# First stage of a two-layer decoder trunk: positions and rope tables first, casts ahead of the block inputs, four more raw buffers, filler matmuls

## The chip, the cores and the metric

The kernel runs on one core of a Trainium2 chip. The metric is the device time of one execution in microseconds (us); the figure used is the median of several executions. The engines of the core are TensorE (PE in the profile, its weight loads PEld), VectorE (DVE), ScalarE (ACT), GpSimd (POOL) and SyncE (SP, which here only issues DMAs).

## What is computed

Two decoder layers on 256 tokens of width 1024, in f32. Each layer modulates its input by a shift and a scale that come from the conditioning vector c, projects it, runs a convolution branch and a retention branch, and then a feed-forward part (dense in layer 0, 8 experts in layer 1).

```python
c_act = jax.nn.silu(c)
for l in range(DEPTH):                                   # DEPTH = 2
    ada = c_act @ w_ada[l] + b_ada[l]
    shift1, scale1, gate1, shift2, scale2, gate2 = [a[:, None, :] for a in jnp.split(ada, N_ADA, axis=-1)]
    h = x * (1.0 + scale1) + shift1
    mix = token_mixer(h, positions, w_in[l], ...)        # proj = h @ w_in; conv_a, conv_b, q, k, v, ... = split(proj)
    x = layer_norm(DEEPNORM_ALPHA * x + gate1 * mix, ln1_g[l], ln1_b[l])
    h = x * (1.0 + scale2) + shift2
    ff = swiglu(h, ...) if l % 2 == 0 else moe_swiglu(h, ...)
    x = layer_norm(DEEPNORM_ALPHA * x + gate2 * ff, ln2_g[l], ln2_b[l])
```

In the mixer, `u = conv_a * sigmoid(conv_b)` feeds the convolution, and q and k are turned by `cos(ang)` and `sin(ang)` with `ang = positions * inv_freq`.

## The kernel before

The weights are streamed once from HBM in units of 128 x 2048 f32 (1 MB), by DMAs that SP issues in the order of the program. They land in a ring of `NWF` = 4 raw buffers `wf`. A weight that TensorE multiplies is split in two halves of 128 x 1024: ScalarE casts the high part (`wh`), VectorE subtracts to get the low part (`wl`), both in rings of `NWS` = 6, and every product is the sum of three matmuls: wh with hH, wh with hL, and wl with hH, where hH and hL are the same two parts of the layer's input. The program is written in a fixed order: `split_to` emits the casts and subtractions some pieces ahead of their use, `issue_dma` emits the next DMA as soon as a raw buffer is free in program order. Each engine runs its own instructions strictly in that order.

The first stage (lines 707 to 717, the loop over `START`) computes conv_a and conv_b of layer 0. Its contraction over 1024 rows is cut into 8 blocks, k = 0 to 7. For block k two units arrive: `adat` (unit a_k) and `s` (unit s_k).

- a_k: VectorE multiplies its two halves by `cb`, the broadcast of silu(c), with a running sum (line 264), which gives shift and scale of the 128 rows of block k in `adac`; line 685 adds the bias.
- `first_h(k)` then makes the modulated input of the block from the transposed x (`xT`). For k = 0 VectorE (line 688), ScalarE (690) and VectorE (691) do it, for k = 1 to 7 GpSimd does all three steps (lines 695, 697, 698).
- s_k is cast and split (lines 1696 and 1698), and `products(k)` (line 674) issues 48 matmuls of 128 x 256: 2 halves, 8 PSUM regions, 3 products. All 8 PSUM banks stay open over the 8 blocks, and after block 7 `A_drain` empties them into `upad`.

Ahead of the stage, `setup` fetches c, makes `cb` with two matmuls and two Silu, and interleaves the DMAs of `cols` (all small per-channel columns), `xT`, `pos` (positions) and the first units. `rope_tables` (from line 1085; VectorE and ScalarE) stands in the program between block 0 and block 1. What follows the stage (`setup_late`, the q and k units `ws`, the units `v` and `g`, and the convolution on VectorE and ScalarE) is the same text in both kernels.

Of the kernel before, what the change touches and what calls it, by code (L numbers as in the profile page):

```python
# [20 lines left out]
P = 128  # L21
T = 256
# [94 lines left out]
def _emit(tc, ctx, a):  # L117
# [6 lines left out]
    small.tile([P, 32], F32, name="padl", bufs=1)  # L124
# [22 lines left out]
    class Unit:  # L147
        kind = None

        def __init__(self, src, n, fn, raw=False, look=LEAD, slot=("stream", "wf", NWF)):  # L150
            self.src, self.n, self.fn, self.raw = src, n, fn, raw
            self.look, self.slot, self.lo = look, slot, {}
            self.issued, self.before = False, None
# [21 lines left out]
    state = {}  # L175
# [275 lines left out]
    def mixer(l, raws, bound, fill=(), tail=()):  # L451
# [4 lines left out]

        def open_pool():
# [8 lines left out]
            R["rH"] = R["p"].tile([P, 16, T], F32R, name="rH")  # L466
            R["rL"] = R["p"].tile([P, 16, T], F32R, name="rL")
            pool.memset(R["upad"][:, :, 0:30], 0.0)
            R["taps"] = col("taps", l * 8 * CK, 8 * CK).rearrange("p (a b) -> p a b", a=8)
# [183 lines left out]
        def S_unit(k):  # L653
            def fn(s, w, wl):
                have.setdefault(k, []).append((w, wl))
                products(k)
            u = Unit(W["s"][k], 2048, fn)
            u.look = 1
            return u

        def products(k):
            if ("h", k) not in have:
                return
            if k == 0 and "A" not in R:
                R["A"] = [mm_bank() for _ in range(4)] + [tp_bank(), tp_bank(), sc_bank(), sc_bank()]
            hi, lo = state["hH"][:, k, :], state["hL"][:, k, :]
            while have.get(k):
                w, wl = have[k].pop(0)
                s = have[k, "s"] = have.get((k, "s"), -1) + 1
                for i in range(8):  # L670
                    o = R["A"][i][:, s * T:(s + 1) * T]
                    ws, wr = w[:, i * P:(i + 1) * P], wl[:, i * P:(i + 1) * P]
                    for n, (p, q) in enumerate(((ws, hi), (ws, lo), (wr, hi))):
                        pe.matmul(o, p, q, start=k == 0 and s == 0 and n == 0, stop=k == 7 and s == 1 and n == 2,
                                  skip_group_check=True)
                    if k == 7 and s == 1:
                        A_drain(i)

        def first_h(k):
            def fn():  # L680
# [5 lines left out]
                f = R["hp"].tile([P, T], F32, name="fh", tag="rot0", bufs=2)  # L686
                if k == 0:
                    dve.tensor_scalar(f, mixc["xT"][:, k, :], adac[:, 0, 8 + k:9 + k], adac[:, 0, k:k + 1],
                                      op0=ALU.mult, op1=ALU.add)
                    act.copy(state["hH"][:, k, :], f)  # L690
                    dve.tensor_tensor(state["hL"][:, k, :], f, state["hH"][:, k, :], op=ALU.subtract)
                    have["h", k] = True
                    products(k)
                    return
                pool.tensor_scalar(f, mixc["xT"][:, k, :], adac[:, 0, 8 + k:9 + k], adac[:, 0, k:k + 1],
                                   op0=ALU.mult, op1=ALU.add)
                pool.tensor_copy(state["hH"][:, k, :], f)
                pool.tensor_tensor(state["hL"][:, k, :], f, state["hH"][:, k, :], op=ALU.subtract)
                have["h", k] = True
                products(k)  # L700
            return fn

        if l == 0:
# [381 lines left out]
    def rope_tables(p):  # L1085
# [20 lines left out]
        dve.scalar_tensor_tensor(n, ang, -1.0, ang, op0=ALU.mult, op1=ALU.max)  # L1106
        dve.tensor_scalar(n, n, -1.0, math.pi / 2, op0=ALU.mult, op1=ALU.add)
        act.activation(cos, n, AF.Sin)
# [559 lines left out]
    def issue_dma(upto=None):  # L1668
        while st["dma"] < (len(units) if upto is None else upto):
# [8 lines left out]
            u.wf = p.tile([P, 2048], F32, name="wf", tag=tag, bufs=bufs)  # L1678
            for o in range(0, u.n, 1024 if u.idx < 2 else u.n):
# [6 lines left out]
    def split_to(i, eng=dve):  # L1686
        while st["split"] <= min(i, len(subs) - 1):
# [3 lines left out]
            if not u.raw:  # L1691
                w = stream.tile([P, 1024], F32R, name="wh", tag="wh", bufs=NWS)
                wl = stream.tile([P, 1024], F32R, name="wl", tag="wl", bufs=NWS)
                m = u.width(s)
                src = u.wf[:, s * 1024:s * 1024 + m]
                act.copy(w[:, 0:m], src)  # L1696
# [132 lines left out]
```

## Time and profile before

| | us |
|---|---|
| median of 3 runs | 1744.8 (1744.21 to 1747.59) |
| profiled execution | 1747.31 |
| its span | 1745.4 |
| PE busy in the span | 1693.2 (97%) |
| DVE busy | 1548.4 (89%) |
| ACT busy | 1159.6 (66%) |
| POOL busy | 53.3 (3%) |

Of 40 equal slices of the span TensorE is busy for 9 tenths or more in all but the first and the last; in the first (0 to 43.6 us) it is 6 tenths. The span is what the profiler recorded from the first instruction to the last; the execution's own time is 1.9 us longer. Matmuls are pipelined, so the distance between two starts tells TensorE's pace better than the duration shown for one of them.

### The profile page before, as it was taken

To read this page: it belongs to the slowest core of one execution; us is meant where nothing else is said; L and a number is where in the kernel's file an instruction comes from. 1 tells how busy PE (TensorE), PEld (TensorE's weight loads), DVE (VectorE), ACT (ScalarE), POOL (GpSimd) and SP (SyncE) were. 2 spreads that over 40 slices of the span, in tenths; PEclk is the share of its full clock that TensorE was granted. 3 is DMA by queue.
4 is the path that set the end of the run, shared out by engine and by line. 5 is a ranking of instruction groups with operands and counts; after the bars stand their busy time and mean duration, and the time that the engine had idled before them with its cause. 6 is when DMAs were issued, how large, how long until landed. Compare 5 with 4: busy or idle time off the path is not lost. (4 is left out here: it accounts for less than half of the span.)

```text
span 1745.4 us, 23910 instructions
## 1 busy us (share of the span) xinstructions
PE 1693.2 (97%) x8896; PEld 1424.0 (82%) x8896; DVE 1548.4 (89%) x2144; ACT 1159.6 (66%) x1634; POOL 53.3 (3%) x50
## 2 busy tenths in 40 slices
PE   6999999999999999999999999999999999999996
PEld 5988877669997798888887788888888888887885
DVE  7699989877787779999878999899999999898996
ACT  3566787644444565667645878778887878787783
POOL 5300000000000000000000000000000000000001
PEclk8999999999999999999999999999999999999998
DMA  9644458876789544455577799899998999898892
GB/s 358 260 164 161 166 208 295 309 294 230 299 303 353 205 171 161 154 192 174 189 301 290 304 333 389 306 383 361 370 363 329 382 354 383 310 393 308 323 351 86
DMA packets 71389, 491.59 MB, mean 282 GB/s; under 512 B 7985, under 2 KB 8753, under 8 KB 14178
## 3 DMA queue, kind: packets, MB, share of 16 engines
q1 hardware_dynamic: 69410, 484.29, 74.0%
q0 software_dynamic: 1568, 5.45, 0.9%
q8 instruction: 72, 1.18, 0.3%
q14 instruction: 51, 0.42, 0.1%
q10 hardware_dynamic: 288, 0.26, 0.0%
HBM read 488.92 MB, written 1.05 MB: 281 GB/s over the span
## 5 line engine op out<-in xcount | busy, mean ns | idle before, releaser
L1698 DVE TENSOR_TENSOR wl<-wf,wh 128x1024 fp32r<-128x1024 f32 x819 | 977.4, 1220 | 80.1 <-ACT wh L1696 66.0
L1696 ACT CAST wh<-wf 128x1024 fp32r<-128x1024 f32 x819 | 840.9, 1049 | 169.3 <-PE ps_mm L140 102.7
L140 PE MATMUL ps_mm<-wh,hgH 128*128 128x512 f32 x704 | 283.5, 403 | 0.0
L140 PE MATMUL ps_mm<-wh,hgL 128*128 128x512 f32 x704 | 275.8, 392 | 0.0
L140 PE MATMUL ps_mm<-wl,hgH 128*128 128x512 f32 x704 | 275.2, 391 | 0.2 <-DVE wl L1698 0.2
L480 ACT ACTIVATE tap<-upad,cols 128x256 f32<-128x256 f32 x300 | 129.6, 501 | 83.9 <-DVE ycv L492 83.8
L140 PE MATMUL ps_mm<-hHn,wh 128*128 128x256 f32 x576 | 163.5, 284 | 0.0
L140 PE MATMUL ps_mm<-hHn,wl 128*128 128x256 f32 x576 | 163.0, 283 | 0.0
L140 PE MATMUL ps_mm<-hLn,wh 128*128 128x256 f32 x576 | 163.0, 283 | 0.0
L140 PEld LDWEIGHTS ps_mm<-wh,hgL 128*128 128x128 f32 x704 | 132.5, 188 | 28.2
L140 PEld LDWEIGHTS ps_mm<-wl,hgH 128*128 128x128 f32 x704 | 132.9, 189 | 26.7 <-issue 1.0
L140 PEld LDWEIGHTS ps_mm<-wh,hgH 128*128 128x128 f32 x704 | 132.6, 188 | 26.0 <-issue 1.0
L140 PE MATMUL ps_mm<-wh,mb 128*128 128x512 f32 (+1 forms) x476 | 145.8, 380 | 0.0
L140 PEld LDWEIGHTS ps_mm<-hHn,wh 128*128 128x128 f32 x576 | 110.6, 192 | 0.4 <-issue 0.2
L140 PEld LDWEIGHTS ps_mm<-hLn,wh 128*128 128x128 f32 x576 | 110.6, 192 | 0.4 <-issue 0.2
L140 PEld LDWEIGHTS ps_mm<-hHn,wl 128*128 128x128 f32 x576 | 110.6, 192 | 0.0
L140 PEld LDWEIGHTS ps_mm<-wh,mb 128*128 128x128 f32 x476 | 87.9, 188 | 17.5 <-issue 1.5
L492 DVE TENSOR_TENSOR ycv<-ycv,tap 128x1024 f32<-128x1024 f32 (+1 forms) x90 | 93.9, 1043 | 5.6 <-ACT tap L480 4.2
L140 PE MATMUL ps_mm<-wl,mb 128*128 128x512 f32 (+1 forms) x238 | 89.8, 377 | 0.0
L140 PE MATMUL ps_mm<-wh,hHn 128*128 128x512 f32 x208 | 84.9, 408 | 0.0
L140 PE MATMUL ps_mm<-wh,hLn 128*128 128x512 f32 x208 | 81.4, 391 | 0.5 <-DVE hLn L392 0.5
L264 DVE SCALAR_TENSOR_TENSOR wf<-wf,cb 128x1024 f32<-128x1024 f32 x64 | 78.1, 1255 | 3.5 <-ACT cb L224 2.0
(306 smaller groups left out, 2851.9 us busy)
## 6 DMA issues: line engine op xcount, KB each, us to landing
wf<-moe_gu SPq DMA_DIRECT2D x176, 1024.0 KB, 7.1
wf<-moe_d SPq DMA_DIRECT2D x75, 1024.0 KB, 6.3
wf<-adat SPq DMA_DIRECT2D x31, 1024.0 KB, 5.9
wf<-ws SPq DMA_DIRECT2D x24, 1024.0 KB, 5.0
wf<-ffn_gu SPq DMA_DIRECT2D x20, 1024.0 KB, 6.1
wf<-v SPq DMA_DIRECT2D x16, 1024.0 KB, 4.9
wf<-g SPq DMA_DIRECT2D x16, 1024.0 KB, 5.0
wf<-f SPq DMA_DIRECT2D x16, 1024.0 KB, 4.9
```

Source lines behind the costliest of these rows:

```text
L140: pe.matmul(out, lhsT, rhs, start=start, stop=stop)
L264: dve.scalar_tensor_tensor(wj, wj, 1.0, state["cb"], op0=ALU.mult, op1=ALU.mult, accum_out=adac[:, l, c0:c0 + 1])
L480: act.activation(t[:, c - c0, :], u[:, c, j:j + T], AF.Copy, scale=taps[:, c, j:j + 1])
L492: dve.tensor_tensor(y, y, prod[j][:, 0:n, :], op=ALU.add)
L1696: act.copy(w[:, 0:m], src)
L1698: eng.tensor_tensor(wl[:, 0:m], src, w[:, 0:m], op=ALU.subtract)
```

## The change

In words:

- `pos` is fetched by the first DMA of ScalarE's queue, and only the first 105 of the 777 columns of `cols` (c, b_ada, inv_freq) are fetched at the start; the other 672 go with unit s_4. `xT` is fetched in pieces of 1, 1, 2 and 4 blocks, ahead of s_0, s_1, s_2 and s_3.
- `rope_tables` is emitted in `setup`, ahead of the bias copy and of a_0. Two of its VectorE steps become one on ScalarE (Abs, and a Sin with bias and scale).
- GpSimd's three steps per block go: ScalarE writes hH straight from `xT` (Identity with scale and bias) and f once more in f32, VectorE subtracts (`low_h`). The low part of block k is emitted after the split of s_k.
- For k of 1 and above, the two casts of s_k stand ahead of hH of block k in ScalarE's order (`early_cast`).
- `products` goes over all 8 regions with one of the three products, then with the next, the one with hL last; only the last half of block 7 keeps the three together.
- a_2, s_2, a_3 and s_3 land in four buffers of their own (the room of rH and rL, which are not in use yet), so that eight units can be under way at first.
- 2 and 9 small matmuls that nobody reads are issued on TensorE around the two that make `cb`.

```diff
+WARM = (2, 9)
+XQ = {0: (0, 1), 1: (1, 2), 2: (2, 4), 3: (4, 8)}
...
     def setup():
...
+        act.dma_start(mixc["pi"], a["pos"].partition_broadcast(P))
         sp.dma_start(row, a["c"])
+        sp.dma_start(cols[:, 0:NCOL0], a["cols"][:, 0:NCOL0])
         pool.memset(one, 1.0)
+        pool.memset(half_pi, math.pi / 2)
+        make_identity(nc, ident)
+        ps = sc_bank()
+        for _ in range(WARM[0]):
+            mm(ps[:, 0:P], one, one, True, True)
         for q in range(2):
             ps = tp_bank()
             mm(ps, one, row[:, q * 512:(q + 1) * 512], True, True)
             act.activation(cb[:, q * 512:(q + 1) * 512], ps, AF.Silu)
-        sp.dma_start(cols, a["cols"])
+        ps = sc_bank()
+        for _ in range(WARM[1]):
+            mm(ps[:, 0:P], ident, ident, True, True)
         st["go"] = True
-        issue_dma(1)
-        sp.dma_start(mixc["xT"][:, 0:2, :], a["xT"][:, 0:2, :])
-        issue_dma(2)
-        sp.dma_start(mixc["pi"], a["pos"].partition_broadcast(P))
-        issue_dma(3)
-        sp.dma_start(mixc["xT"][:, 2:8, :], a["xT"][:, 2:8, :])
-
-        make_identity(nc, ident)
+        issue_dma(8)
+        rope_tables(state["hp0"], half_pi)
...
         def S_unit(k):
             def fn(s, w, wl):
+                if ("f", k) in R:
+                    split_to(st["cur"] + 1)
+                    low_h(k, R.pop(("f", k)))
...
-                for i in range(8):
+                end = k == 7 and s == 1
+                turns = [(i, n) for i in range(8) for n in range(3)] if end else \
+                    [(i, n) for n in range(3) for i in range(8)]
+                for i, n in turns:
                     o = R["A"][i][:, s * T:(s + 1) * T]
...
+                    p, q = ((w, hi), (wl, hi), (w, lo))[n]
...
+        def early_cast(u):
+            for s in range(2 if u.issued else 0):
+                w = stream.tile([P, 1024], F32R, name="wh", tag="wh", bufs=NWS)
+                wl = stream.tile([P, 1024], F32R, name="wl", tag="wl", bufs=NWS)
+                act.copy(w, u.wf[:, s * 1024:(s + 1) * 1024])
+                u.w[s] = (w, wl)
...
+                xk, s, b = mixc["xT"][:, k, :], adac[:, 0, 8 + k:9 + k], adac[:, 0, k:k + 1]
+                act.activation(state["hH"][:, k, :], xk, AF.Identity, bias=b, scale=s)
                 if k == 0:
...
-                pool.tensor_scalar(f, mixc["xT"][:, k, :], adac[:, 0, 8 + k:9 + k], adac[:, 0, k:k + 1],
-                                   op0=ALU.mult, op1=ALU.add)
-                pool.tensor_copy(state["hH"][:, k, :], f)
-                pool.tensor_tensor(state["hL"][:, k, :], f, state["hH"][:, k, :], op=ALU.subtract)
...
+                    act.activation(f, xk, AF.Identity, bias=b, scale=s)
+                    R["f", k] = f
...
+        def low_h(k, f):
+            dve.tensor_tensor(state["hL"][:, k, :], f, state["hH"][:, k, :], op=ALU.subtract)
...
+                    if k == 4:
+                        u.pre = lambda: sp.dma_start(cols[:, NCOL0:], a["cols"][:, NCOL0:])
+                if k1:
+                    u.pre = lambda k0=k0, k1=k1: sp.dma_start(mixc["xT"][:, k0:k1, :], a["xT"][:, k0:k1, :])
+                if k in (2, 3):
+                    u.slot = ("mix0", f"r{'HL'[k - 2]}{int(what == 's')}", 1)
+                if what == "s" and k:
+                    prog.insert(len(prog) - 1, lambda u=u: early_cast(u))
                 prog.append(u)
```

How the rows of the engines move is shown at three places. The first is SP's DMAs at the start of the program, each with its target and source (`wf<-adat` is a unit a_k, `wf<-s` a unit s_k). Before:

```order
L219 DMA cstt<-c 1x1024
L225 DMA cols<-cols 128x777
L1681 DMA wf<-adat 128x1024 x2
L228 DMA xT<-xT 128x512
L1681 DMA wf<-s 128x1024 x2
L230 DMA cos<-pos 128x256
L1681 DMA wf<-adat 128x2048
L232 DMA xT<-xT 128x1536
L1681 DMA wf<-s 128x2048
```

And in the changed kernel (the positions are now the first row of ScalarE's queue, `L223 DMA cos<-pos 128x256`):

```order
L224 DMA cstt<-c 1x1024
L225 DMA cols<-cols 128x105
L1712 DMA wf<-adat 128x1024 x2
L739 DMA xT<-xT 128x256
L1712 DMA wf<-s 128x1024 x2
L1712 DMA wf<-adat 128x2048
L739 DMA xT<-xT 128x256
L1712 DMA wf<-s 128x2048
L1712 DMA wf<-adat 128x2048
L739 DMA xT<-xT 128x512
L1712 DMA wf<-s 128x2048
```

Ahead of s_1 (the second whole `wf<-s`) there are now the small part of `cols` and two pieces of `xT` of one block each, where the whole of `cols` and of `xT` stood.

The second place is ScalarE's order in the first blocks. Before, hH of block 0, the casts of s_0, the tables, and then nothing but casts (15 of them, to the drains):

```order
L224 ACTIVATE cb<-ps_tp 128x512 x2
L690 CAST hH_127<-fh 128x256
L1696 CAST wh<-wf 128x1024 x2
L1104 ACTIVATE sin<-ang 128x256
L1105 ACTIVATE sin<-sin 128x256
L1108 ACTIVATE cos<-nrot 128x256
L1696 CAST wh<-wf 128x1024 x15
```

In the changed kernel (`L700` is `early_cast`, `L712` hH and `L717` f of a block):

```order
L235 ACTIVATE cb<-ps_tp 128x512 x2
L1134 ACTIVATE sin<-ang 128x256
L1135 ACTIVATE sin<-sin 128x256
L1136 ACTIVATE nrot<-ang 128x256
L1137 ACTIVATE cos<-nrot,padl 128x256
L712 ACTIVATE hH_164<-xT,adac 128x256
L1730 CAST wh<-wf 128x1024 x2
L700 CAST wh<-wf 128x1024 x2
L712 ACTIVATE hH_164<-xT,adac 128x256
L717 ACTIVATE fh<-xT,adac 128x256
```

The tables now come before everything of block 0, and from block 1 on hH and f of a block stand behind both casts of its weights.

The third place is VectorE's order from block 0 to the multiplications of a_2. Before:

```order
L691 TENSOR_TENSOR hL_128<-fh,hH_127 128x256
L1698 TENSOR_TENSOR wl<-wf,wh 128x1024 x2
L1090 CAST ang<-cos 128x256
L1091 TENSOR_SCALAR ang<-ang,cols 128x256
L1093 TENSOR_SCALAR nrot<-ang 128x256
L1094 TENSOR_SCALAR nrot<-nrot 128x256
L1101 SCALAR_TENSOR_TENSOR ang<-nrot,ang 128x256 x4
L1103 TENSOR_SCALAR ang<-ang 128x256
L1106 SCALAR_TENSOR_TENSOR nrot<-ang 128x256
L1107 TENSOR_SCALAR nrot<-nrot 128x256
L264 SCALAR_TENSOR_TENSOR wf,adac<-wf,cb 128x1024 x2
L685 TENSOR_TENSOR adac<-adac,adab 128x2
```

In the changed kernel (the eight table rows stand ahead of `adab`, at the very start; `L271` is the multiplication of an a unit):

```order
L722 TENSOR_TENSOR hL_165<-fh,hH_164 128x256
L1732 TENSOR_TENSOR wl<-wf,wh 128x1024 x2
L271 SCALAR_TENSOR_TENSOR wf,adac<-wf,cb 128x1024 x2
L709 TENSOR_TENSOR adac<-adac,adab 128x2
L1732 TENSOR_TENSOR wl<-wf,wh 128x1024 x2
L722 TENSOR_TENSOR hL_165<-fh,hH_164 128x256
L271 SCALAR_TENSOR_TENSOR wf,adac<-wf,cb 128x1024 x2
```

Between the split of s_0 and the multiplications of a_1 nothing stands any more, and each block has one more VectorE row of 128 x 256 (`L722`) behind its split.

## Rows read from the trace of the kernel before

**Rows 1.** Stretches: length, busy us per engine (PE first), PEclk, DMA, GB/s.

```profile
12.87:21.40 8.53, 8.07 (x48) 7.63 (x48) 8.18 (x16) 3.41 (x6) 0.00 (x0) 1.00 1.01 419
21.40:28.79 7.39, 0.65 (x3) 0.29 (x2) 7.32 (x12) 2.79 (x3) 6.54 (x4) 0.71 0.97 380
28.79:34.70 5.91, 5.91 (x27) 5.91 (x28) 5.88 (x8) 2.00 (x2) 5.76 (x3) 0.50 1.01 381
34.70:71.70 37.00, 37.00 (x311) 37.00 (x310) 25.43 (x35) 11.39 (x15) 25.32 (x16) 1.00 0.84 322
...
90.00:110.00 20.00, 17.88 (x76) 13.57 (x75) 19.90 (x30) 14.41 (x25) 0.00 (x0) 1.00 0.47 161
```

**Rows 2.** Waits from 0 to 72 us: who, for whom, total, times, longest.

```profile
ACT wh L1696 <- DMA wf<-s: 18.8, 8, 3.4
...
DVE upad L646 <- ACT th L645: 10.4, 3, 10.1
...
PE ps_mm L674 <- POOL hH L697: 5.6, 1, 5.6
```

**Rows 3.** Timeline of PE: the two matmuls for cb, the last of block 7.

```profile
2.40 3.75 PE L140 MATMUL ps_tp<-cstt,sel 1*128 1x512 f32 x4 [2.40 <-DMA cstt<-c]
...
71.58 0.28 PE L674 MATMUL ps_sc<-hH,wl 128*128 128x256 f32 x1
```

**Rows 4.** Timeline of ACT: the first casts of s_1 to s_4.

```profile
20.21 1.99 ACT L1696 CAST wh<-wf 128x1024 fp32r<-128x1024 f32 x2 [0.24 <-DMA wf<-s]
...
25.19 1.99 ACT L1696 CAST wh<-wf 128x1024 fp32r<-128x1024 f32 x2 [2.99 <-DMA wf<-s]
...
30.24 2.00 ACT L1696 CAST wh<-wf 128x1024 fp32r<-128x1024 f32 x2 [3.06 <-DMA wf<-s]
...
35.24 1.05 ACT L1696 CAST wh<-wf 128x1024 fp32r<-128x1024 f32 x1 [3.00 <-DMA wf<-s]
```

**Rows 5.** Timeline of DVE and ACT: a_0, hL, tables, a_1, a_2.

```profile
6.82 1.23 DVE L264 SCALAR_TENSOR_TENSOR wf<-wf,cb 128x1024 f32<-128x1024 f32 x1 [2.00 <-ACT cb L224]
...
9.55 1.22 DVE L264 SCALAR_TENSOR_TENSOR wf<-wf,cb 128x1024 f32<-128x1024 f32 x1 [1.50 <-DMA wf<-adat]
...
11.90 0.43 DVE L691 TENSOR_TENSOR hL<-fh,hH 128x256 fp32r<-128x256 f32 x1 [0.47 <-ACT hH L690]
...
15.23 0.28 DVE L1090 CAST ang<-cos 128x256 f32<-128x256 int32 x1
...
18.43 0.29 DVE L1103 TENSOR_SCALAR ang<-ang 128x256 f32<-128x256 f32 x1
...
18.76 0.42 ACT L1104 ACTIVATE sin<-ang 128x256 f32<-128x256 f32 x1 [4.71 <-DVE ang L1103]
...
19.43 1.22 DVE L264 SCALAR_TENSOR_TENSOR wf<-wf,cb 128x1024 f32<-128x1024 f32 x1
...
24.19 1.22 DVE L264 SCALAR_TENSOR_TENSOR wf<-wf,cb 128x1024 f32<-128x1024 f32 x1
```

**Rows 6.** Groups of GpSimd's instructions from 0 to 62 us: busy us, mean ns.

```profile
L695 POOL TENSOR_SCALAR fh<-xT,adac 128x256 f32<-128x256 f32 x7 | 18.1, 2591 | 20.4 <-DVE adac L685 20.4
L698 POOL TENSOR_TENSOR hL<-fh,hH 128x256 fp32r<-128x256 f32 x7 | 10.4, 1479 | 0.6
L697 POOL CAST hH<-fh 128x256 fp32r<-128x256 f32 x7 | 9.2, 1316 | 0.5
```

**Rows 7.** DMA from 0 to 75 us: 40 slices of 1.875 us; KB, median us to landing.

```profile
GB/s 2 232 242 347 350 430 427 416 425 423 419 415 253 419 428 406 336 415 376 380 411 354 310 406 419 385 406 354 358 415 376 345 409 408 398 35 0 0 0 4
...
wf<-s SPq DMA_DIRECT2D x7, 1024.0 KB, 6.7
...
wf<-v SPq DMA_DIRECT2D x2, 1024.0 KB, 5.5
...
cols<-cols SPq DMA_DIRECT2D x1, 388.5 KB, 3.1
```

**Rows 8.** Timeline of SP: the last units issued inside the stage.

```profile
54.66 3.15 SPq L1681 DMA_DIRECT2D wf<-v  x2
```

More of the change, by code (lines that the diff above doesn't have):

```diff
@@ L123, in _emit @@
     small = ctx.enter_context(tc.tile_pool(name="small", bufs=4))
-    small.tile([P, 32], F32, name="padl", bufs=1)
+    padl = small.tile([P, 32], F32, name="padl", bufs=1)
     ctx.enter_context(tc.manual_schedule())
@@ L152, in __init__ @@
             self.look, self.slot, self.lo = look, slot, {}
-            self.issued, self.before = False, None
+            self.issued, self.before, self.pre = False, None, None
         def width(self, s):
@@ L455, in mixer, with open_r @@
         S = {}
+        def open_r():
+            for q in "HL":
+                R["r" + q] = Parts([(8 * n, R["p"].tile([P, 8, T], F32R, name=f"r{q}{n}", tag=f"r{q}{n}"))
+                                    for n in range(2)])
         def open_pool():
@@ L465, in open_pool @@
             R["p"].tile([P, 16], F32, name="padr")
-            R["rH"] = R["p"].tile([P, 16, T], F32R, name="rH")
-            R["rL"] = R["p"].tile([P, 16, T], F32R, name="rL")
+            if l:
+                open_r()
+            else:
+                state["mix0"] = R["p"]
             pool.memset(R["upad"][:, :, 0:30], 0.0)
@@ L661, in products @@
         def products(k):
-            if ("h", k) not in have:
-                return
             if k == 0 and "A" not in R:
@@ L669, in products @@
                 s = have[k, "s"] = have.get((k, "s"), -1) + 1
-                for i in range(8):
+                end = k == 7 and s == 1
+                turns = [(i, n) for i in range(8) for n in range(3)] if end else \
+                    [(i, n) for n in range(3) for i in range(8)]
+                for i, n in turns:
                     o = R["A"][i][:, s * T:(s + 1) * T]
[L672 to L676, printed above, removed]
-                        A_drain(i)
+                    p, q = ((w, hi), (wl, hi), (w, lo))[n]
+                    pe.matmul(o, p[:, i * P:(i + 1) * P], q, start=k == 0 and s == 0 and n == 0, stop=end and n == 2,
+                              skip_group_check=True)
+                    if end and n == 2:
+                        A_drain(i)
+        def early_cast(u):
[4 more added lines that the diff above has]
+                u.w[s] = (w, wl)
         def first_h(k):
@@ L1105, in rope_tables @@
         act.activation(sin[:, 1, :], sin[:, 0, :], AF.Copy, scale=-1.0)
-        dve.scalar_tensor_tensor(n, ang, -1.0, ang, op0=ALU.mult, op1=ALU.max)
-        dve.tensor_scalar(n, n, -1.0, math.pi / 2, op0=ALU.mult, op1=ALU.add)
-        act.activation(cos, n, AF.Sin)
+        act.activation(n, ang, AF.Abs)
+        act.activation(cos, n, AF.Sin, bias=half_pi, scale=-1.0)
     def moe():
@@ L1678, in issue_dma @@
             u.wf = p.tile([P, 2048], F32, name="wf", tag=tag, bufs=bufs)
+            if u.pre is not None:
+                u.pre()
             for o in range(0, u.n, 1024 if u.idx < 2 else u.n):
@@ L1691, in split_to @@
             if not u.raw:
-                w = stream.tile([P, 1024], F32R, name="wh", tag="wh", bufs=NWS)
-                wl = stream.tile([P, 1024], F32R, name="wl", tag="wl", bufs=NWS)
                 m = u.width(s)
                 src = u.wf[:, s * 1024:s * 1024 + m]
-                act.copy(w[:, 0:m], src)
+                if s in u.w:
+                    w, wl = u.w[s]
+                else:
+                    w = stream.tile([P, 1024], F32R, name="wh", tag="wh", bufs=NWS)
+                    wl = stream.tile([P, 1024], F32R, name="wl", tag="wl", bufs=NWS)
+                    act.copy(w[:, 0:m], src)
                 eng = u.lo.get(s, eng)
```

29 lines of the change are left out of this document (13 added, 16 removed).

## Prediction

> **What bounds the kernel now.** I first read the busy time by stretch [rows 1]. TensorE is the engine that sets the end: outside the first stage it is busy nearly always, so what the stage is worth is read from when TensorE leaves it. The last matmul of block 7 starts at 71.58 [rows 3], the next unit's at 71.70. The stage holds 8 x 48 = 384 matmuls. The rows give two paces: 311 in 37.00 us from 34.70 on, 0.12 us each, where the granted clock is 1.00 (2.4 GHz), and 27 in 5.91 us, 0.22 us each, where it is 0.50 (1.2 GHz). At the fast pace a block is 48 x 0.12 = 5.76 us and the stage 46.1 us; it took 71.7 - 12.87 = 58.8. The 12.7 us between are visible: block 0 needs 8.53 us instead of 5.76, then 7.39 us hold only 3 matmuls, and then 27 matmuls go at half pace, 5.91 us instead of 3.24 (2.7 + 7.2 + 2.7 = 12.6).
>
> Second, the waits [rows 2]. The hole is a wait for GpSimd's hH (5.6 us) and what follows from it. After it TensorE runs without a gap from 28.79 to 71.70, so everything behind block 1 is late only because block 1 was late and cold. The other engines are ahead: ScalarE waits for the DMA of s in 8 places (18.8 us), and VectorE has nothing to do for 10.1 us before the first drain.
>
> Third, why block 1 was late. Its a_1 was multiplied by VectorE only at 19.43, behind the rope tables that begin at 15.23 [rows 5]; then came GpSimd's first two steps, 2.59 + 1.32 us on average [rows 6]. Its weights were there at 20.21 [rows 4].
>
> Fourth, the DMAs, since they become the limit. s_1 to s_4 land at 20.21, 25.19, 30.24 and 35.24 [rows 4], about 5.0 us for a pair of units (2.1 MB), and their share is 0.97 to 1.01 in these stretches [rows 1]: the stream is saturated.
>
> **When the weights of each block land.** I add up bytes in issue order and compare with the GB/s of the slices [rows 7]. The first five slices carry 2.20 MB by 9.4 us; the next six run at 423 GB/s. Ahead of and with s_1 there were 5.78 MB (cols 0.40, two a, two s at 1.05 each, xT 1.05, pos 0.13): 9.4 + 3.58 / 0.423 = 17.8 us, and the row says 20.21, so landing lags the count by 2.4 us. In the changed order it is 4.65 MB (pos 0.13, cols 0.05, four units 4.20, two pieces of xT 0.26): 9.4 + 5.8 + 2.4 = 17.6 us. Then s_2 with 2.36 MB more at 23.1, s_3 with 2.62 MB more at 29.3, s_4 with 2.44 MB more at 35.1. That last one is 35.24 before: by s_4 the same bytes have passed, and the change in order only brings the first blocks forward. The four extra raw buffers cannot make a saturated stream faster; I give them nothing.
>
> **When each block can start.** Behind s_k's landing ScalarE has two casts (2.0 us, [rows 4]) and hH (0.42, the size of the Sin row of 128 x 256, [rows 5]): 2.4 us. The multiplications of a_1 run in VectorE's free time, from about 15 to 17.5, so they are not last any more. Block 1 can start at 20.0, block 2 at 25.5, block 3 at 31.7, block 4 at 37.5. TensorE at the fast pace is free from block 1 at 25.8, from block 2 at 31.5, from block 3 at 37.5. The two chains are within 0.3 us of each other up to block 4; from there the units land faster (about 5 us a pair) than TensorE eats them (5.76): block 4 at 37.5, 5 at 43.2, 6 at 49.0, 7 at 54.8, end 60.5. **TensorE leaves the stage at 60.5 instead of 71.7: 11.2 us earlier.**
>
> **What each edit costs, and its cover.**
> - Tables first: 15.23 to 18.72 is 3.5 us of VectorE [rows 5], now beside the start, where VectorE has almost nothing before 6.82. They need pos and the small cols. Whole cols took 3.1 us to land [rows 7]; the smaller part and pos should be there at 2.5 to 4.3 us, so the tables and the bias copy (0.5) end between 6.5 and 8.3. a_0's second half lands about 0.7 us before the old 9.55 (0.21 MB less ahead of it). So a_0 is done between 0.7 us earlier and as before, and block 0 starts at 11.9 to 12.9. At the fast pace it ends by 19, ahead of the 20.0 of block 1: hidden. If the cover goes (pos late by over 2 us), block 1 slips by what is over.
> - Low part on VectorE: 0.43 us a block more [rows 5]. A block's turn was 24.19 - 19.43 = 4.76 us while GpSimd was mostly idle; 5.2 with it, under 5.76: hidden. GpSimd's work (2.59 + 1.32 + 1.48 us a block, [rows 6]) disappears; it costs nothing and its removal is the 5.6 us wait above. ScalarE goes to 2.0 + 0.84 us a block: hidden.
> - The order of products: inside a block the low part of the input is wanted 16 matmuls (1.9 us) after the start, about 4.3 us after s_k's landing, and ready at 3.9. Nothing.
> - hH behind the casts: the 0.42 us already counted. Queued behind the casts' DMA wait on ScalarE stand only hH and f of the same block.
> - The rest of `cols` and of `xT` lands ahead of s_2 to s_4, counted above in bytes; the first use of the taps is behind the stage.
> - Filler matmuls: TensorE is empty until c lands at 2.40, and from the end of the cb matmuls (2.40 + 3.75 = 6.15, [rows 3]) to block 0. Those two have 512 columns and take 1.87 us each, so one of 128 columns takes about 0.47, nine take 4.2, and they end by 10.4. On the path: nothing. What they may give is block 0 at the fast pace. TensorE ran block 0 partly at half pace before, 8.53 us in all.
>
> **Is it given back?** Behind the stage TensorE needs ws_0 to ws_1 and v. The last v units are issued from 54.66 [rows 8] and land 5.5 us later [rows 7], about 63, while they are wanted two units after the stage, at 60.5 + 11.5 = 72. VectorE bounds part of what comes next (19.90 of 20 us, [rows 1]), but its work there starts with the drains, and in its idle 10.1 us it did none of it ahead; so that stretch moves as a whole. Later DMAs wait for free buffers and move too.
>
> **Sum.** The profiled execution is 1747.31 us with a span of 1745.4, its median 2.5 below it. 1745.4 - 11.2 = 1734.2 span, 1736.1 for that execution, and **1733.6 us against the median of 1744.8**. Bounds: if landing were no limit at all, block 0 would end at 18.0 and the stage at 18.0 + 40.3 = 58.3: gain 13.4, 1731.4. If the landing of s_1 does not move at all (20.21), block 1 starts at 22.6 and the stage ends at 62.9: gain 8.8, 1736.0.
>
> **Rivals.**
> 1. *Eight units under way land later one by one.* With a deeper queue the 2.4 us lag could grow. For it: the lag is there. Against it: it is the same for s_1 and s_2. Each us at s_4 is a us at the end: 2 to 4 us more give 1736 to 1738.
> 2. *The fillers do not raise the clock, or the gap before block 1 loses it.* Block 0 at 0.22 us a matmul lasts 10.5 us, to 22.4 to 23.4: 2.4 to 3.4 us lost; a further loss costs the 2.7 us seen in [rows 1]. 1736 to 1739.
> 3. *The stage ends earlier, but TensorE then waits for a DMA or a drain and nothing is left:* 1743 to 1746. It needs ws_1 or v about 10 us later than their landing above.
> 4. *Slower: the clock falls in the gap before every block.* A cold block costs 48 x 0.10 = 4.8 us, so 2.4 of them eat the 11.2; with 4 cold, 1744.8 - 11.2 + 19 = 1753. Against it: a cold block outlasts the arrival of the next, so the gaps close, and in [rows 1] TensorE without gaps came back to 1.00 after one. What fell was after a hole of over 5 us; I expect at most 2.
>
> Rival 4 is what the Trainium skill describes in "TensorE: Matmul & The Clock Gate", section "HAM oscillation": a kernel whose work per weight tile is shorter than the wait for the next one falls back to the low clock at every tile. By that rule every block would be cold, which is this rival at its worst. The trace bears out the fall (0.71, then 0.50, after the hole) but not a repeat: the blocks here outlast the wait for the next.
>
> **Numbers.** Forecast with its own range (1731 to 1736) 0.58; rival 1 0.14; rival 2 0.14; rival 3 0.08; rival 4 0.06. The 8 in 10 range takes the forecast and most of rivals 1 and 2: 1731 to 1739. No change means within 0.2%, 3.5 us, which is about what a measurement of this kernel can tell: 1741.3 to 1748.3. Forecast and rivals 1 and 2 lie below that: faster 0.86, same 0.08, slower 0.06.
>
> **What would show it.** The first casts of s_1 at 17.6 and of s_4 near 35; matmuls of block 0 at 0.12 us; a gap of 2 us before block 1, which starts near 20, and none over 0.5 after block 4; the last matmul of the stage near 60.5; GpSimd idle; the stretch behind the stage with the same lengths, 11 us earlier. It is wrong if s_1 or s_4 land later than that by more than 3 us, if the granted clock in the stage is 0.50 for more than one block, or if a new wait stands between the drains and the convolution.

## The result, and the profile after

| | before | after |
|---|---|---|
| median of 6 executions each | 1745.93 us (1744.21 to 1748.11) | 1735.74 us (1733.81 to 1737.29) |
| profiled execution, its span | 1747.31, 1745.4 us | 1735.97, 1734.2 us |
| TensorE leaves the first stage | 71.70 us | 61.23 us |
| last DMA issue (the output) | 1738.92 us | 1727.38 us |

The ratio is 0.9941 with a 95% interval of 0.9931 to 0.9951: the kernel became faster by 10.2 us, and the first stage ends 10.5 us earlier. The forecast was 1733.6 in a range of 1731 to 1739.

The stretches of the changed kernel (columns as in [rows 1]) are block 0 in two parts, blocks 1 to 7, and two stretches well behind the stage:

```profile
12.98:16.10 3.12, 3.12 (x14) 3.12 (x15) 3.12 (x3) 0.90 (x1) 0.00 (x0) 0.50 1.02 423
16.10:20.20 4.10, 4.10 (x36) 4.10 (x35) 4.07 (x8) 3.00 (x4) 0.00 (x0) 1.00 1.02 418
20.20:61.20 41.00, 40.60 (x338) 40.40 (x337) 33.75 (x55) 20.89 (x30) 0.00 (x0) 1.00 1.00 397
85.00:90.00 5.00, 2.99 (x9) 2.37 (x10) 5.00 (x8) 4.09 (x8) 0.00 (x0) 0.78 0.15 43
90.00:95.00 5.00, 5.00 (x23) 4.19 (x22) 5.00 (x9) 3.42 (x7) 0.00 (x0) 0.88 0.66 215
```

The two bad stretches of [rows 1], 7.39 us with 3 matmuls and 5.91 us at half pace, are gone. What is left is half pace at the start of block 0, which stood in the 8.53 us of [rows 1] too: 14 matmuls in 3.12 us at the low level (0.50, 1.2 GHz). From 20.20 on TensorE idles for 0.4 of 41 us. GpSimd does nothing. The last two lines are new: TensorE is fed thinly there in both kernels, but here the clock falls to 0.78 and 0.88, where [rows 1] has 1.00 behind the stage.

The waits up to 62 us, beside [rows 2]:

```profile
ACT wh L700 <- DMA wf<-s: 18.7, 7, 4.6
DVE ang L1120 <- DMA cos<-pos: 4.6, 1, 4.6
PE ps_mm L691 <- ACT wh L1730: 3.1, 1, 3.1
PE ps_mm L691 <- ACT hH L712: 0.4, 1, 0.4
```

The 5.6 us that TensorE waited for GpSimd's hH are gone. What remains is 3.1 us before block 0 and 0.4 us before block 3. ScalarE's 18.7 us of waiting for s are harmless as long as TensorE has a block in hand.

TensorE's timeline shows the fillers, block 0, blocks 1 and 3, the last matmul and the next unit ([rows 3]):

```profile
6.02 3.81 PE L143 MATMUL ps_sc<-ident 128*128 128x128 f32 x18
12.98 1.23 PE L691 MATMUL ps_mm<-hH,wh 128*128 128x256 f32 x4 [3.14 <-ACT wh L1730]
20.21 0.64 PE L691 MATMUL ps_mm<-hH,wh 128*128 128x256 f32 x4
32.30 0.74 PE L691 MATMUL ps_mm<-hH,wh 128*128 128x256 f32 x4 [0.40 <-ACT hH L712]
61.12 0.28 PE L691 MATMUL ps_sc<-hL,wh 128*128 128x256 f32 x1
61.23 0.28 PE L143 MATMUL ps_mm<-hH,wh 128*128 128x256 f32 x1
```

ScalarE's timeline has the first casts of s_1 to s_4 ([rows 4]) and hH of block 1:

```profile
16.45 2.00 ACT L700 CAST wh<-wf 128x1024 fp32r<-128x1024 f32 x2 [2.58 <-DMA wf<-s]
18.36 0.60 ACT L712 ACTIVATE hH<-xT,adac 128x256 fp32r<-128x256 f32 x1
22.11 2.00 ACT L700 CAST wh<-wf 128x1024 fp32r<-128x1024 f32 x2 [2.65 <-DMA wf<-s]
29.75 2.00 ACT L700 CAST wh<-wf 128x1024 fp32r<-128x1024 f32 x2 [4.65 <-DMA wf<-s]
35.55 2.00 ACT L700 CAST wh<-wf 128x1024 fp32r<-128x1024 f32 x2 [2.81 <-DMA wf<-s]
```

VectorE's timeline has the first table row, a_0, a_1, the low part of block 1, a_2 and the low part of block 3 ([rows 5]):

```profile
4.60 0.29 DVE L1120 CAST ang<-cos 128x256 f32<-128x256 int32 x1 [4.60 <-DMA cos<-pos]
8.79 1.22 DVE L271 SCALAR_TENSOR_TENSOR wf<-wf,cb 128x1024 f32<-128x1024 f32 x1
15.24 1.22 DVE L271 SCALAR_TENSOR_TENSOR wf<-wf,cb 128x1024 f32<-128x1024 f32 x1
20.00 0.42 DVE L722 TENSOR_TENSOR hL<-fh,hH 128x256 fp32r<-128x256 f32 x1
20.34 1.22 DVE L271 SCALAR_TENSOR_TENSOR wf<-wf,cb 128x1024 f32<-128x1024 f32 x1
33.10 0.42 DVE L722 TENSOR_TENSOR hL<-fh,hH 128x256 fp32r<-128x256 f32 x1
```

s_1 is cast at 16.45 instead of 20.21, s_4 at 35.55, where it was (35.24). a_1 is multiplied at 15.24 instead of 19.43, so from block 1 on the weights are the last of a block's inputs to come. The tables are not free, though: a_0 begins at 8.79 instead of 6.82, because pos lands at 4.60.

SP's timeline shows what becomes of the gain behind the stage ([rows 8] has v). Before:

```profile
75.23 2.60 SPq L1681 DMA_DIRECT2D wf<-g  x2
120.68 7.98 SPq L1681 DMA_DIRECT2D wf<-ws  x2
1738.92 2.88 SPq L1607 DMA_DIRECT2D o<-zg  x4
```

And in the changed kernel:

```profile
51.85 2.80 SPq L1712 DMA_DIRECT2D wf<-v  x2
65.08 2.60 SPq L1712 DMA_DIRECT2D wf<-g  x2
112.08 7.98 SPq L1712 DMA_DIRECT2D wf<-ws  x2
1727.38 2.87 SPq L1636 DMA_DIRECT2D o<-zg  x4
```

The lead over the kernel before is 10.15 us at g, 8.6 us at the `ws` pair of 112.08, and 11.5 us at the end.

### The profile page after: what moved, and what is told of

Read it like the earlier page. It is cut to its first block, busy times and chain, and to the rows that moved or that the text cites. A ratio compares the mean times of both kernels' runs of the same rounds, so it can differ in the third digit from the quotient of the medians.

```text
span 1734.2 us, 23941 instructions
## 1 busy us (share of the span) xinstructions
PE 1694.4 (98%) x8918; PEld 1425.9 (82%) x8918; DVE 1545.2 (89%) x2149; ACT 1166.6 (67%) x1649; POOL 15.7 (1%) x30
## 5 line engine op out<-in xcount | busy, mean ns | idle before, releaser
L1730 ACT CAST wh<-wf 128x1024 fp32r<-128x1024 f32 x805 | 826.4, 1050 | 146.4 <-PE ps_mm L143 100.3
L143 PE MATMUL ps_mm<-wl,hHn 128*128 128x512 f32 x208 | 81.0, 390 | 0.0
```

The lines of the kernel that those rows point to most:

```text
L143: pe.matmul(out, lhsT, rhs, start=start, stop=stop)
```

## The experiments

The theory: the stage is a chain of the weights' landing and TensorE's 5.76 us a block, and the edits matter only as far as they let block 1 start near 20 us. Rivals: the four buffers or the fillers do it, or the tables alone. All runs are in one table; medians are compared with executions of the kernel before on the same chip. The change itself took 1735.74 and, run again in another job, 1739.15 us (e11), with stage ends of 61.23 and 61.26. So the stage's end is the measure of an edit here; totals of different jobs are not ranked within 3 us or so.

| run | stage ends, us | median, us (executions) | ratio to before [95%] |
|---|---|---|---|
| the change | 61.23 | 1735.74 (6) | 0.9941 [0.9931, 0.9951] |
| e1, no fillers | 61.34 | 1736.87 (4) | 0.9951 [0.9935, 0.9968] |
| e2, four buffers | 61.22 | 1737.00 (4) | 0.9949 [0.9932, 0.9965] |
| e3, GpSimd back | 65.75 | 1742.53 (10) | 0.9981 [0.9971, 0.9990] |
| e4, casts behind hH | 70.09 | 1746.53 (10) | 1.0003 [0.9990, 1.0016] |
| e5, tables back | 63.00 | 1738.68 (5) | 0.9967 [0.9953, 0.9981] |
| e6, old fetch | 63.45 | 1737.34 (7) | 0.9958 [0.9944, 0.9972] |
| e7, 17 fillers | 61.27 | 1738.95 (8) | 0.9969 [0.9958, 0.9980] |
| e8, tables alone | 68.09 | 1745.53 (10) | 1.0002 [0.9992, 1.0012] |
| e9, late fetch, 17 fillers | 60.31 | 1739.76 (6) | 0.9964 [0.9952, 0.9976] |
| e10, late fetch, no fillers | 60.95 | 1734.46 (5) | 0.9940 [0.9927, 0.9953] |
| e11, the change again | 61.26 | 1739.15 (5) | 0.9964 [0.9951, 0.9977] |
| e12, e10 again | 60.79 | 1734.23 (5) | 0.9940 [0.9923, 0.9958] |

**e1, no fillers.**

```diff
-WARM = (2, 9)
+WARM = (0, 0)
```

> The changed kernel without its 2 + 9 filler matmuls. In the changed kernel block 0 starts at 12.98 us, runs at half pace (granted clock 0.50) up to 16.06 and ends at 20.2; the stage ends at 61.2. Theory A (weights' landing and TensorE's 5.76 us a block bound the stage, fillers are idle work): block 0 starts at the same time; its clock comes up at most as late as in the kernel before (4.6 us after its start instead of 3.1), so block 0 ends at most 0.7 us later; the holes of 0.5 us before blocks 3 and 4 take most of that up: stage end 61.2 to 61.9, total within 0.7 us of the changed kernel. Rival (the fillers are what brings the clock up): block 0 wholly at half pace, ends at 23.3, and the stage ends at 63.6 to 64.3, total 2.5 to 3 us slower than the changed kernel.

Block 0 now runs at half pace to 18.1 us and ends at 21.0 (20.2 with the fillers), a little worse than theory A had it (5.2 us at half pace for 4.6 at most, 0.8 us lost for 0.7), and the stage ends 0.1 us later, within theory A. TensorE's timeline, and two stretches (columns as in [rows 1]):

```profile
12.95 1.22 PE L691 MATMUL ps_mm<-hH,wh 128*128 128x256 f32 x4 [6.73 <-ACT wh L1730]
```

```profile
12.95:16.50 3.55, 3.55 (x16) 3.55 (x17) 3.55 (x5) 0.90 (x1) 0.00 (x0) 1.00 1.03 423
18.00:20.00 2.00, 2.00 (x19) 2.00 (x18) 1.85 (x2) 2.00 (x4) 0.00 (x0) 1.00 1.06 427
```

Both stretches show a granted clock of 1.00, yet the first has 16 matmuls in 3.55 us, 0.22 each, and the second 19 in 2.00, 0.11 each. So the pace is the witness here, not the clock's column. The 0.8 us that the fillers win in block 0 are lost again: blocks 1 to 7 take 61.23 - 20.21 = 41.0 us in the change, most of the excess before block 3, and 61.34 - 21.02 = 40.3 here, without any hole. TensorE only waits longer for weights.

**e2, four raw buffers as before.**

```diff
-                if k in (2, 3):
-                    u.slot = ("mix0", f"r{'HL'[k - 2]}{int(what == 's')}", 1)
```

> The changed kernel with the four raw buffers of the ring alone (a_2, s_2, a_3 and s_3 in the ring too). Theory A (the DMA stream is saturated, the extra buffers only deepen its queue): s_1 lands at 16.4 and s_4 at 35.5 within 1 us of the changed kernel, the stage ends at 61.2 to 62, total equal within 1 us. Rival (it is the deeper queue that brings the weights forward): s_2 to s_4 land 2 to 4 us later, the stage ends at 63 to 65, total 2 to 4 us slower.

The stage ends where it did, and s_1 and s_4 are cast at 16.64 and 35.53 (16.45 and 35.55 with eight): the buffers give nothing, and the deeper queue costs nothing.

**e3, GpSimd makes the block inputs again.**

```diff
-                    act.activation(f, xk, AF.Identity, bias=b, scale=s)
-                    R["f", k] = f
+                    pool.tensor_scalar(f, xk, s, b, op0=ALU.mult, op1=ALU.add)
+                    pool.tensor_copy(state["hH"][:, k, :], f)
+                    pool.tensor_tensor(state["hL"][:, k, :], f, state["hH"][:, k, :], op=ALU.subtract)
```

> The changed kernel with f, hH and hL of blocks 1 to 7 on GpSimd again, as in the kernel before; tables, fetches, casts and the order of products as in the changed kernel. Theory A: hH comes 3.9 us behind the bias add of a block (2.59 + 1.32) instead of within 1.2, and VectorE's rows take 1.4 to 1.8 us instead of 1.2 while GpSimd works; block 1 can start at 17.6 + 4.0 = 21.7 instead of 20.2, VectorE's turn is about 5.7 us a block, and the stage ends at 62.5 to 64: total 1.5 to 3 us slower than the changed kernel, that is, most of the gain over the kernel before stays. Rival (GpSimd's three steps are what made the kernel before late): the stage ends at 68 to 72, most of the 10 us is gone.

65.75 lies between the two theories. GpSimd's timeline and the timeline of TensorE say why:

```profile
17.92 3.57 POOL L717 TENSOR_SCALAR fh<-xT,adac 128x256 f32<-128x256 f32 x1 [16.21 <-DVE adac L709]
29.39 0.56 POOL L717 TENSOR_SCALAR fh<-xT,adac 128x256 f32<-128x256 f32 x1
42.41 3.57 POOL L717 TENSOR_SCALAR fh<-xT,adac 128x256 f32<-128x256 f32 x1 [3.68 <-DVE adac L709]
```

```profile
22.87 0.74 PE L691 MATMUL ps_mm<-hH,wh 128*128 128x256 f32 x4 [2.07 <-POOL hH L718]
47.36 0.74 PE L691 MATMUL ps_mm<-hH,wh 128*128 128x256 f32 x4 [1.20 <-POOL hH L718]
54.14 0.74 PE L691 MATMUL ps_mm<-hH,wh 128*128 128x256 f32 x4 [0.76 <-POOL hH L718]
```

The same step takes 0.56 us while VectorE idles (28.6 to 30.85) and 3.57 us beside its splits and multiplications. The mean of 2.59 in [rows 6] hid two prices, and the expectation had used it. In the kernel before, the step of block 1 took the high one:

```profile
22.11 3.57 POOL L695 TENSOR_SCALAR fh<-xT,adac 128x256 f32<-128x256 f32 x1 [20.41 <-DVE adac L685]
```

In e3 TensorE waits 4.0 us for hH in three places.

**e4, casts behind hH, in the units' own place.**

```diff
-                if what == "s" and k:
-                    prog.insert(len(prog) - 1, lambda u=u: early_cast(u))
```

> The changed kernel without early_cast: hH and f of a block stand ahead of the casts of its weights on ScalarE. Theory A1 (the split on VectorE is what is delayed): from the bias add to the subtraction VectorE now waits for hH, f and a cast, 0.6 + 0.5 + 1.05 us, so its turn grows from 5.2 to 7.5 us a block, above TensorE's 5.76; the last bias add comes at 17.6 + 6 x 7.5 = 62.6, the stage ends near 70 to 71, total 9 to 10 us slower than the changed kernel, about as slow as the kernel before. Rival A2 (ScalarE is half idle, its order does not matter, and hH ahead of the casts lets TensorE start after one cast): stage end 60.5 to 61.2, total equal or up to 0.7 us faster.

With this one line of order undone the stage ends at 70.09, as theory A1 had it, and in the total nothing of the gain is left (ratio 1.0003). ScalarE's timeline:

```profile
24.93 0.60 ACT L712 ACTIVATE hH<-xT,adac 128x256 fp32r<-128x256 f32 x1 [4.30 <-DVE adac L709]
25.92 1.98 ACT L1728 CAST wh<-wf 128x1024 fp32r<-128x1024 f32 x2
32.20 0.60 ACT L712 ACTIVATE hH<-xT,adac 128x256 fp32r<-128x256 f32 x1 [4.30 <-DVE adac L709]
```

hH of a block waits for VectorE's `adac`; behind it stand the casts; for the casts waits VectorE's split; and only behind the split stands the next `adac`. That ring takes 32.20 - 24.93 = 7.27 us a block, more than TensorE's 5.76, in every block from the second on. ScalarE waits for `adac` 30.9 us in 8 places and never for a DMA of s.

The order is therefore not a gain over the kernel before that stands by itself. There ScalarE had only casts from block 1 on, and no such ring. It came with hH's move from GpSimd to ScalarE, and `early_cast` is what that move needs.

**e5, tables behind s_0 again.**

```diff
-        rope_tables(state["hp0"], half_pi)
...
+                if what == "s" and k == 0:
+                    code(lambda: rope_tables(state["hp0"], state["padl"][:, 0:1]))
```

> The changed kernel with rope_tables emitted between block 0 and block 1 again (in its new form, positions still first on ScalarE's queue). Theory A (what counts is whether hH of a block is ready before its weights and TensorE): a_0 starts at 6.8 instead of 8.8, block 0 near 12; the tables then take VectorE 3.2 us behind the split of s_0, a_1 ends near 20.0 instead of 17.7, block 1 starts at 20.8 instead of 20.2, and from block 3 on, which waits for s_3 at 29.7 + 2.5, everything is as in the changed kernel: stage end 61.2 to 62.0, total within 0.8 us of it. Rival (the tables' 3.5 us are on the path to every later block): stage end 63.5 to 65, total 2.5 to 4 us slower.

TensorE's timeline, and two stretches (columns as in [rows 1]):

```profile
11.12 0.74 PE L690 MATMUL ps_mm<-hH,wh 128*128 128x256 f32 x4 [1.49 <-ACT wh L1731]
21.11 0.74 PE L690 MATMUL ps_mm<-hH,wh 128*128 128x256 f32 x4 [3.69 <-ACT hH L711]
```

```profile
20.00:24.00 4.00, 2.89 (x19) 2.89 (x20) 4.00 (x6) 3.54 (x5) 0.00 (x0) 0.82 0.99 410
24.00:28.00 4.00, 4.00 (x28) 4.00 (x28) 3.97 (x7) 1.09 (x2) 0.00 (x0) 0.76 1.02 416
```

Block 0 starts 1.9 us earlier and at full pace, and then block 1 is 0.9 us later behind a hole of 3.69 us; the granted clock fell behind that hole (0.82 in 20 to 24, 0.76 in 24 to 28). The expectation of 61.2 to 62.0 had left that fall out; no hole follows, and the stage ends at 63.00. The tables' place is worth 1.8 us.

**e6, the old order of the fetches.**

```diff
-XQ = {0: (0, 1), 1: (1, 2), 2: (2, 4), 3: (4, 8)}
+XQ = {0: (0, 2), 1: (2, 8)}
...
-        sp.dma_start(cols[:, 0:NCOL0], a["cols"][:, 0:NCOL0])
+        sp.dma_start(cols, a["cols"])
...
-                    if k == 4:
-                        u.pre = lambda: sp.dma_start(cols[:, NCOL0:], a["cols"][:, NCOL0:])
```

> The changed kernel with the old sizes of the first fetches: all 777 columns of cols at the start, xT in pieces of 2 (ahead of s_0) and 6 blocks (ahead of s_1); positions stay first on ScalarE's queue. Theory A (bytes ahead of s_1 set its landing): s_1 lands near 19.3 to 20.2 instead of 16.4, s_4 unchanged near 35.5; block 1 starts at 21.8 to 22.7, TensorE then has no hole up to the end: stage end 62.2 to 63.2, total 1 to 2 us slower than the changed kernel. Rival (the order of the fetches does not matter, VectorE's turn does): stage end 61.2 to 61.6.

s_1 is cast at 19.82, 3.4 us later than in the change, and block 0 starts at 14.89, 1.9 us later; the stage ends 2.2 us later, just above what was expected. s_4, expected unchanged near 35.5, is cast at 36.38. ScalarE's timeline:

```profile
19.82 2.00 ACT L700 CAST wh<-wf 128x1024 fp32r<-128x1024 f32 x2 [4.03 <-DMA wf<-s]
```

**e7, seventeen fillers.**

```diff
-WARM = (2, 9)
+WARM = (2, 17)
```

> The changed kernel with 17 instead of 9 matmuls of the identity behind the two for cb, so that TensorE works on nearly to block 0. What they cost: at half pace 0.42 us each they would end near 13.2, at full pace near 11.5. Theory A: the granted clock does not fall ahead of block 0, block 0 ends near 19 instead of 20.2, block 1 starts at 19.0, but block 3 still waits for s_3 (29.7 + 2.5): the stage ends at 61.2 as before, total equal within 0.5 us. Rival (TensorE alone bounds the stage): the 1.2 us reach the end, stage end 60.0.

TensorE's timeline:

```profile
12.71 0.74 PE L691 MATMUL ps_mm<-hH,wh 128*128 128x256 f32 x4 [0.53 <-ACT wh L1730]
25.98 0.74 PE L691 MATMUL ps_mm<-hH,wh 128*128 128x256 f32 x4 [1.19 <-ACT hH L712]
32.31 0.75 PE L691 MATMUL ps_mm<-hH,wh 128*128 128x256 f32 x4 [0.31 <-ACT hH L712]
```

These fillers reach to 12.2, and block 0 runs at full pace (over by 18.9). It gives nothing: block 3 starts at 32.31, as in the change (32.30), since s_3 is cast at 29.76 (29.75). The total of 1738.95 is 3.2 us above the change's first median, where 0.5 at most was expected, and 0.2 below its second (e11).

**e8, the tables first, alone, on the kernel before.**

```diff
+        act.dma_start(mixc["pi"], a["pos"].partition_broadcast(P))
         sp.dma_start(row, a["c"])
...
         issue_dma(2)
-        sp.dma_start(mixc["pi"], a["pos"].partition_broadcast(P))
         issue_dma(3)
+        rope_tables(state["hp0"])
...
-                    if k == ROPE:
-                        code(lambda: rope_tables(R["hp"]))
```

> The kernel before with one part of the change alone: positions fetched first on ScalarE's queue and rope_tables (old form) ahead of a_0; GpSimd's steps, the old fetch sizes, the old casts and products stay. Theory A (block 1 was late by VectorE's tables and by GpSimd's steps, one after the other): a_1 is done near 19 instead of 21.9, GpSimd's hH and hL near 23 and 25 instead of 27.0 and 28.7, the hole is about 3 to 4 us shorter and TensorE may keep its clock; stage end 65 to 68 instead of 71.7, total 4 to 6.5 us faster than the kernel before. Rival (the tables only trade places, the delay moves to a_0 and block 0): stage end 70 to 72, total equal within 2 us.

The profiled execution leaves the stage 3.6 us earlier and takes 1742.8, but the median is that of before. Both miss the expectation (stage end 65 to 68, total 4 to 6.5 us faster), the first by 0.1 us. Ten executions fall in two groups, four from 1741.55 to 1743.55 and six from 1745.32 to 1747.58. The mean granted clock of an execution was 0.994 to 0.996 in the first group and 0.991 to 0.994 in the second, so the second ran more of its time at the low level. Where, was not seen: the profiled execution is one of the first group. The tables alone are therefore not the change.

**e9 and e10, a later fetch.** If landing is the limit behind block 1, then xT in eight pieces and the rest of `cols` with s_7 should bring s_3 and s_4 forward. e9 has 17 fillers, e10 none.

```diff
-XQ = {0: (0, 1), 1: (1, 2), 2: (2, 4), 3: (4, 8)}
+XQ = {k: (k, k + 1) for k in range(8)}
...
-                    if k == 4:
-                        u.pre = lambda: sp.dma_start(cols[:, NCOL0:], a["cols"][:, NCOL0:])
...
+                        if k0 == 7:
+                            sp.dma_start(cols[:, NCOL0:], a["cols"][:, NCOL0:])
```

> The changed kernel with 17 identity matmuls, xT in eight pieces (one ahead of each s_k) and the rest of cols ahead of s_7. Theory A (landing of s_3 and s_4 and the pace of block 0 bound the stage together, each alone hides the other): 0.39 MB less ahead of s_3 and 0.74 MB less ahead of s_4 let them land near 28.7 and 33.9 instead of 29.7 and 35.5; with block 0 at full pace the stage ends at 59.8 to 60.2 instead of 61.2, 1 to 1.4 us, if nothing behind the stage changes. Rival (a single bound): stage end 61.2 as with either edit alone.

> The same late fetches without any filler matmul. Theory A: block 0 ends at 20.2 to 20.6 as without fillers, TensorE has no hole any more, the stage ends at 20.4 + 40.5 = 60.9, 0.3 to 0.5 us ahead of the changed kernel. Rival (the landings alone bound the stage): 59.8, as with fillers.

s_3 is cast at 28.54 and 27.46, s_4 at 33.89 and 33.51 (29.75 and 35.55 in the change). e10 has no hole from block 0 to the end of the stage and ends it at 60.95, as expected; e9 ends at 60.31 with one hole of 0.79 us, 0.1 us past theory A's range. So the landings and block 0's pace bound the stage together: with the later fetch the fillers are worth 0.5 to 0.6 us (60.31 against 60.95 and, in e12, 60.79), without it nothing. In the total e9 is no better than e7, and e10 has the lowest median of its job. Its two stretches behind the stage keep a clock of 1.00:

```profile
85.00:90.00 5.00, 3.29 (x14) 2.74 (x15) 5.00 (x8) 4.38 (x8) 0.00 (x0) 1.00 0.18 31
90.00:95.00 5.00, 5.00 (x25) 4.21 (x24) 5.00 (x9) 3.43 (x7) 0.00 (x0) 1.00 0.65 223
```

**e11 and e12, once more.** The change unedited, on the chip of e9 and e10, and e10 in another job.

> The changed kernel again, on the chip of the two runs beside it, so that they can be compared with it: stage end 61.2 within 0.2 us in the profile; the total within 2 us of 1735.7, since the places behind the stage at which the granted clock falls differ from execution to execution.

> The kernel with late fetches and no fillers once more, since it came out 4.7 us faster than the changed kernel beside it although its stage ends only 0.3 us earlier (60.95 against 61.26). Theory B (the rest is where the granted clock happens to fall behind the stage, which differs from execution to execution): stage end 60.9 again within 0.2 us, total 1735 to 1738, not clearly apart from the 1735.7 and 1739.2 of the changed kernel. Rival (the edit itself keeps the clock up behind the stage): 1733.5 to 1735.5 again, no stretch between 80 and 600 us below a granted clock of 1.00 in the profile.

Beside e10 the change took 1739.15, and all five executions of e10 (1733.33 to 1736.01) lie below its five (1737.43 to 1741.76). So e11 missed its expectation of 1735.7 within 2 us, with the stage's end as expected. e12 (1734.23, stage end 60.79, no stretch of 20 us between 80 and 600 us under 1.00) came out as its rival had it, and not at the 1735 to 1738 of theory B. Over both jobs the change has 11 executions from 1733.8 to 1741.8, and e10 with e12 ten from 1732.2 to 1737.7. Side by side the late fetch without fillers is 4.7 us under the change, of which 0.3 us are in the stage; measured against the kernel before, e10 and e12 (0.9940) equal the change's first job (0.9941), so a gain in the total is shown in one job only. The rest of the 4.7 us is behind the stage; e11's lead over before falls from 10.1 us at g to 8.6 at 112 us and is 8.4 at the end, e10's grows from 10.4 to 12.8. The mean granted clock of an execution was 0.993 to 0.996 in all five of e10 and 0.990 to 0.992 in all five of e11. An estimate from the two means, 0.9948 and 0.9912: 0.0036 of 1737 us is 6 us of full clock, enough for the 4.4 us behind the stage.

## Why the prediction was right, step by step

- **The landings** came as counted, within 1.2 us: casts of s_1 to s_4 at 16.45, 22.11, 29.75 and 35.55 for 17.6, 23.1, 29.3 and 35.1. e2 and e6 show that it is the bytes ahead of a unit that set them, not the buffers. Rival 1 did not happen. A hit within 1.2 us is no finer than the spread, though: with the same fetches s_2 was cast from 21.95 (e11) to 23.43 (e7).
- **Block 1** started at 20.21 for 20.0, but for another reason: its hH was ready at 18.96, and TensorE was not free. Block 0 began at 12.98, just past the late end of the forecast, because pos landed at 4.60 and the first columns of `cols` at 5.30, and ran its first part at half pace. So the gap of 2 us before block 1 did not exist. s_1 came 1.2 us before its count, and block 0 ended 1.2 us past the 19 that was its latest forecast; that block 1 met its 20.0 all the same is luck. That is rival 2 in part: the nine fillers ended at 9.83, TensorE stood empty for 3.1 us and began at 0.50. It cost next to nothing in the end (e7).
- **The stage's end**, 61.23 for 60.5, is the term that was too optimistic. 0.6 us arose at block 3, which started at 32.30 for 31.7: s_3 came 0.45 us late, and hH takes 0.60, not the 0.42 of the Sin row; 0.1 us came after it.
- **The edits' covers.** The low part on VectorE is hidden: its turn is 20.34 - 15.24 = 5.10 us, for 5.2. Buffers are worth nothing in the stage (e2), and nor are the fillers as long as block 3 waits for s_3 (e1, e7). Taken out of the changed kernel one at a time, GpSimd's removal is worth 4.5 us (e3), the fetch order 2.2 (e6), the tables' place 1.8 (e5), and the order on ScalarE 8.9 (e4), which is the price of the ring and no part of the 10.5. The values can't be added up, since each was measured with all the others in place. The prediction put GpSimd and tables first and had not priced the casts' place by itself. The order of the products was taken out in no run: by the trace hL of block 3 is ready at 33.10 + 0.42 = 33.52, 1.2 us behind the block's first matmul at 32.30, and in the old order the second matmul asks for it, so by estimate it saves about 1.1 us there.
- **Two readings were off** without a part in the sum: block 1's steps on GpSimd took 3.57 + 1.26 us in the kernel before and not the mean 2.59 + 1.32, and the hole's share of the 12.7 us is 7.39 - 3 x 0.12 = 7.0 and not 7.2.
- **Given back:** nothing by a wait, so rival 3 fell. But the stretch behind the stage did not move quite rigidly: the lead went 10.15, 8.6, 11.5 us. The first loss stands where the granted clock fell (0.78 and 0.88), which the prediction had at nothing. All 13 profiles of edited kernels agree on it: from g to the next `ws` pair but one (112.08 in the change) the lead shrinks by 1.55 us in the change, 1.56 in e11, 1.59 in e9 and 1.57 in e8, the four in which the clock fell there, and by 0.02 at most in the other nine.
- **The total.** The median is 2.1 us above the 1733.6: 1.1 us is the kernel before, whose median rose from 1744.8 to 1745.93 with three more executions, and 1.0 us a gain of 10.2 for 11.2, of which the stage explains 0.7. The span met its 1734.2 by luck: the 0.7 us missing in the stage came back behind it in this execution. And the same kernel in another job took 1739.15 (e11), just outside the 1731 to 1739, with the same stage.
- **Rival 4**, the clock falling before every block, did not come: 20.20 to 61.20 has 1.00. The Trainium skill's section "HAM oscillation" ("TensorE: Matmul & The Clock Gate") speaks of work per tile that is shorter than the wait for the next. That case did not arise here: from block 1 on TensorE waits 0.4 us at most ahead of 5.76 us of work, so the prediction's "by that rule every block would be cold" read too much into it. The low level came once, behind the 3.1 us in which TensorE stood empty, and cost part of one block.

**Open:** why the clock falls behind the stage in some kernels. In the profiled executions it fell at 85 to 95 us in the change, e11 (0.80 and 0.86 in the two halves) and e9, and at 90 to 100 us in e8, and not in e1 to e7, e10 and e12; neither the fillers nor the buffers sort these. The two kernels that were profiled twice did the same both times (the change and e11 fell, e10 and e12 did not), which speaks for a habit of the kernel and is too little to show it. e2 and e7 kept 1.00 there and still ended with leads of 6.7 and 10.0 us, so more is lost in other places.

## What to carry to other kernels

On an engine that runs strictly in order, put what waits only for a DMA ahead of what waits for another engine: here hH ahead of the casts closed a ring over two engines and cost 8.9 us of the stage (e4). A step that moves to another engine needs a new place in that engine's order. When the stream is saturated, count the bytes that stand ahead of the first needed unit and move the others behind it (2.2 us, e6); more buffers did not help (e2). Before warming TensorE up, ask what the block after next waits for: a faster first block only waited longer here (e7).

## What the runs showed of the hardware

- GpSimd's 128 x 256 multiply-add in f32 took 0.56 us alone and 3.57 us beside VectorE (e3). The Trainium skill ("GPSIMD Engine Reference", section "1. Specifications") says that its SBUF interfaces are shared with VectorE and contended by VectorE instructions with two SBUF inputs; this trace agrees, since the slow steps stand beside VectorE's splits and multiplications, and it puts a factor of 6 on it.
- The granted clock reads 1.00 in e1 from 12.95 on, while the matmuls run at 0.22 us each until 18: there the column does not show what TensorE got. [rows 1] has the same 1.00 over block 0, which took 8.53 us for 48 matmuls.
- With the same instructions on TensorE up to there, block 0 ran at half pace until 18.1 in e1 and until 17.2 in e10.
- The executions of the change spread over 8 us (1733.8 to 1741.8), as much as most edits here were worth. A low mean granted clock goes with a long time where two groups can be told apart (e8; e10 beside e11). One fall behind the stage cost 1.5 to 1.6 us, in four profiles out of 13.
